# Average pooling over 512 MB: the first load issued as 16 rows and 112 rows

## The chip, the cores and the metric

The kernel runs on one core of a Trainium2 chip. The metric is device time in microseconds (us) of one execution; lower is better. Before the change it is 1552.77 us, the median of 3 runs (1552.75 to 1552.84).

## What is computed

The input x has shape (64, 256, 8192) in float32, which is 536.87 MB. The window and the stride are both 4, so the windows do not overlap, and every output is the mean of four neighbouring numbers of its row:

```
out_len = (length - kernel_size) // stride + 1
for i in range(out_len):
    start = i * stride
    output[:, :, i] = np.mean(x[:, :, start : start + kernel_size], axis=2)
```

The output is (64, 256, 2048) in float32, 134.22 MB. Each input byte is read once, and there are three additions and one multiplication for each output.

## The kernel before, in words

Since 8192 is a multiple of 4, no window crosses the end of a row, and the kernel treats x as one flat array. It cuts it into 64 blocks of 128 x 16384 numbers (`xb`, 8.39 MB each): 128 rows, one for each partition of the on-chip memory, and 64 KB in each row. The rows of a block follow one another in DRAM without gaps. There are two input buffers, `xt0` and `xt1`, each of which holds one block, and two output buffers, `ot0` and `ot1`, each of which holds the results of two blocks.

Four queues do the work, and the order on each of them is written out by hand, with semaphores between them:

- **SP** issues the loads (`load`, L61 to L64), at first blocks 0 and 1, one right after the other with no wait between (L69 and L70). After that it issues the load of block i+2 into the buffer of block i once VectorE has read that buffer (semaphore `free`). Each load adds 16 to the semaphore `full[k]` of its buffer.
- **VectorE (DVE)** waits for `full[k]`, adds neighbours (L75: 16384 numbers of each row to 8192, into the first half of the same buffer) and adds neighbours again (L77: to 4096, into the output buffer).
- **ScalarE (ACT)** multiplies two blocks' sums by 1/4 at a time (L93), and its DMA queue stores them (L96, `stored[q]`).
- After 60 blocks in the loop (L115 on) four blocks follow one by one. The last one is loaded in two halves (`TAIL`, L112), so that the last additions and the last store are short.

The DMA work is done by 16 DMA engines that all queues share. The trace records each packet that they move. Of a load of 128 rows there are 128 packets of 65536 bytes, one for each row, eight for each engine; of a store of two blocks there are 256 packets of 16384 bytes.

At the start, before the loop, SP's two loads stand in front of the barrier that all engines pass on the way in (L71). The first wait of VectorE in the loop is the one for `full[0]`.

Of the kernel before, what the change touches and what calls it, by code (L numbers as in the profile page):

```python
# [1 line left out]

# [4 lines left out]


FULL = 16384
PAIR = 2  # L10
ROUND = 2 * PAIR

TAIL = (8192, 8192)


@with_exitstack
def kernel(
    ctx: ExitStack,
    tc: tile.TileContext,
    x: bass.AP,  # L20
    kernel_size: bass.AP,
    stride: bass.AP,
    out: bass.AP,
):
    nc = tc.nc
    K, S = int(kernel_size), int(stride)
    assert K == S == 4
    B, C, L = x.shape
    assert L % K == 0
    P = nc.NUM_PARTITIONS  # L30
    dt = x.dtype
    add, mult = mybir.AluOpType.add, mybir.AluOpType.mult

    M = FULL // K
    blocks = B * C * L // P // FULL
    loop = blocks - ROUND
    assert blocks * P * FULL == B * C * L and blocks % ROUND == 0 and sum(TAIL) == FULL
    xb = x.rearrange("b c l -> (b c l)").rearrange("(n p m) -> n p m", p=P, m=FULL)
    ob = out.rearrange("b c l -> (b c l)").rearrange("(n p m) -> p n m", p=P, m=M)


    xt0 = ctx.enter_context(nc.sbuf_tensor([P, FULL], dt))
    xt1 = ctx.enter_context(nc.sbuf_tensor([P, FULL], dt))
    ot0 = ctx.enter_context(nc.sbuf_tensor([P, PAIR * M], dt))
    ot1 = ctx.enter_context(nc.sbuf_tensor([P, PAIR * M], dt))
    xt, ot = [xt0, xt1], [ot0, ot1]


    full = [nc.alloc_semaphore(f"full{k}") for k in range(2)]
    piece = [nc.alloc_semaphore(f"piece{k}") for k in range(len(TAIL))]  # L50
    free = nc.alloc_semaphore("free")
    summed = nc.alloc_semaphore("summed")
    summed_last = nc.alloc_semaphore("summed_last")
    scaled = nc.alloc_semaphore("scaled")
    scaled_last = nc.alloc_semaphore("scaled_last")
    stored = [nc.alloc_semaphore(f"stored{k}") for k in range(2)]

    def take(engine, sem, n):
        engine.wait_ge(sem, n).then_inc(sem, -n)  # L59

    def load(i, k):  # L61
        d = nc.sync.dma_start(out=xt[k][:, :], in_=xb[i])
        d.then_inc(full[k], 16)
        return d  # L64

    for k in range(2):
        tc.no_tile_sem_insts.add(load(k, k).ins.name)  # L69
    tc.close()  # L70
    tc.compile()  # L71

    def sums(t, o):
        w = t.shape[1]
        nc.vector.tensor_tensor(out=t[:, : w // 2], in0=t[:, ::2], in1=t[:, 1::2], op=add)  # L75
        nc.vector.drain()
        return nc.vector.tensor_tensor(  # L77
            out=o, in0=t[:, : w // 2 : 2], in1=t[:, 1 : w // 2 : 2], op=add
        )

    def pair(i, q, ahead):

        for k in range(PAIR):
            take(nc.vector, full[k], 16)
            if k == 0:
                take(nc.vector, stored[q], 16)
            sums(xt[k][:, :], ot[q][:, k * M : (k + 1) * M]).then_inc(free, 1)
            take(nc.sync, free, 1)
            if k == 1:
                nc.sync.sem_inc(summed, 1)  # L90
            ahead(k)
        take(nc.scalar, summed, 1)
        nc.scalar.mul(ot[q][:, :], ot[q][:, :], 1.0 / K).then_inc(scaled, 1)  # L93
        take(nc.scalar, scaled, 1)
        o = ot[q][:, :].rearrange("p (n m) -> p n m", n=PAIR)
        nc.scalar.dma_start(out=ob[:, bass.ds(i, PAIR), :], in_=o).then_inc(stored[q], 16)  # L96


    zero = nc.const_aps.tensor(0.0, [P, 1], dt)
    nc.scalar.mul(ot[0][:, :1], zero, 1.0).then_inc(stored[0], 16)  # L100
    nc.scalar.sem_inc(stored[1], 16)

    edges = [sum(TAIL[:i]) for i in range(len(TAIL) + 1)]
    pieces = list(zip(edges[:-1], edges[1:]))
    xe, oe = xb[blocks - 1], ob[:, blocks - 1, :]

    def ahead_of_last(k):
        if k == 0:
            load(blocks - 2, 0)
        else:  # L110
            for sem, (a, b) in zip(piece, pieces):
                nc.sync.dma_start(out=xt[1][:, a:b], in_=xe[:, a:b]).then_inc(sem, 16)  # L112

    engines = (mybir.EngineType.SP, mybir.EngineType.DVE, mybir.EngineType.Activation)
    with nc.Fori(0, loop // ROUND, 1, engines=engines) as r:  # L115
        for q in range(2):
            i = r * ROUND + q * PAIR
            pair(i, q, lambda k: load(i + (PAIR + k), k))

    for k in range(PAIR):
        o = ot[0][:, k * M : (k + 1) * M]
        take(nc.vector, full[k], 16)
        if k == 0:
            take(nc.vector, stored[0], 16)
        sums(xt[k][:, :], o).then_inc(free, 1)
        take(nc.sync, free, 1)
        nc.sync.sem_inc(summed, 1)
        ahead_of_last(k)  # L130
        take(nc.scalar, summed, 1)
        if k == 0:
            nc.scalar.mul(o, o, 1.0 / K).then_inc(scaled, 1)  # L133
            take(nc.scalar, scaled, 1)
            nc.scalar.dma_start(out=ob[:, loop, :], in_=o).then_inc(stored[0], 16)
        else:
            nc.scalar.mul(o, o, 1.0 / K).then_inc(scaled_last, 1)  # L137
            take(nc.sync, scaled_last, 1)
            nc.sync.dma_start(out=ob[:, loop + 1, :], in_=o).then_inc(stored[0], 16)

    take(nc.vector, stored[1], 16)
    take(nc.vector, full[0], 16)
    o = ot[1][:, :M]
    sums(xt[0][:, :], o).then_inc(summed_last, 1)
    take(nc.scalar, summed_last, 1)
    nc.scalar.mul(o, o, 1.0 / K).then_inc(scaled_last, 1)  # L146
    take(nc.sync, scaled_last, 1)
    nc.sync.dma_start(out=ob[:, blocks - 2, :], in_=o).then_inc(stored[1], 16)


    for sem, (a, b) in zip(piece, pieces):
        o = ot[1][:, M + a // K : M + b // K]
        take(nc.vector, sem, 16)
        sums(xt[1][:, a:b], o).then_inc(summed_last, 1)
        take(nc.scalar, summed_last, 1)
        nc.scalar.mul(o, o, 1.0 / K).then_inc(scaled, 1)  # L156
        take(nc.scalar, scaled, 1)
        nc.scalar.dma_start(out=oe[:, a // K : b // K], in_=o).then_inc(stored[1], 16)
    take(nc.sync, stored[0], 32)
    take(nc.sync, stored[1], 16 * (1 + len(TAIL)))  # L160


# [1 line left out]
_INS = ['x', 'kernel_size', 'stride']  # L164
_OUTS = [((64, 256, 2048), 'float32')]

_NUMBERS = {'kernel_size': 4, 'stride': 4}


# [26 lines left out]
```

## Time and profile before

| what | value |
|---|---|
| median of 3 runs | 1552.77 us |
| the profiled execution | 1553.16 us |
| its span, from the first to the last instruction | 1551.8 us |
| around the span | 1.36 us |
| DVE busy | 839.9 us (54%) |
| ACT busy | 227.0 us (15%) |
| DMA, queue of SP (q1), share of 16 engines | 80.5% |
| DMA, queue of ACT (q10), share of 16 engines | 19.6% |
| first load issued by SP | 0.74 us |
| first packet of it starts | 1.77 us |
| its 16 completions | 22.03 to 22.86 us |
| first DVE instruction | 23.11 us |

The times of single events are counted from the start of the span. A transfer has landed when all 16 of its completions, one of each DMA engine, have come in. A packet is put down with its whole size at one moment, so that windows of a few us can show more than the engines can move; windows of 10 us and more do not suffer much from that.

### The profile page before, as it was taken

What the parts mean: (1) busy time and instruction counts of PE and PEld (TensorE: products, weight loads), DVE (VectorE), ACT (ScalarE), POOL (GpSimd) and SP (SyncE); (2) the same over time, 40 slices, a digit from 0 to 9 for tenths busy, and PEclk for the clock granted to TensorE, in tenths of its full rate; (3) what the DMA queues carried; (4) which work ended last, traced back from release to release, by engine and by line L of the source; (5) the groups of instructions that cost most, each with busy time, mean ns of one, the idle gap of its engine ahead of it and who ended that gap; (6) DMA issues with size and microseconds to landing.
All of it is one profiled execution on the core that took longest, in us unless ns stands there. A gap on an engine that the chain in (4) does not pass through costs nothing. (4 is left out here: it accounts for less than half of the span.)

```text
span 1551.8 us, 942 instructions
## 1 busy us (share of the span) xinstructions
DVE 839.9 (54%) x130; ACT 227.0 (15%) x37; POOL 0.2 (0%) x4
## 2 busy tenths in 40 slices
DVE  3645646456465564654646546455464554645546
ACT  0111011110111101111011110111101111011111
POOL 0000000000000000000000000000000000000000
DMA  9999999999999999999999999999999999999999
GB/s 414 419 444 441 417 439 432 439 441 416 433 432 439 446 434 417 432 433 446 439 436 434 413 440 439 439 432 438 414 439 439 432 439 438 416 437 432 439 432 413
DMA packets 18240, 671.10 MB, mean 432 GB/s; under 512 B 1600, under 2 KB 1600, under 8 KB 1600
## 3 DMA queue, kind: packets, MB, share of 16 engines
q1 hardware_dynamic: 9648, 541.07, 80.5%
q10 hardware_dynamic: 8592, 130.03, 19.6%
HBM read 536.87 MB, written 134.22 MB: 432 GB/s over the span
## 5 line engine op out<-in xcount | busy, mean ns | idle before, releaser
L75 DVE TENSOR_TENSOR xt<-xt 128x8192 f32<-128x8192 f32 (+1 forms) x65 | 556.5, 8561 | 699.4 <-DVEq L59 699.4
L93 ACT ACTIVATE ot<-ot 128x8192 f32<-128x8192 f32 x30 | 210.9, 7029 | 1246.2 <-ACTq L59 1246.2
L77 DVE TENSOR_TENSOR ot<-xt 128x4096 f32<-128x4096 f32 (+1 forms) x65 | 283.4, 4360 | 4.9
L146 ACT ACTIVATE ot<-ot 128x4096 f32<-128x4096 f32 x1 | 3.6, 3616 | 20.6 <-ACTq L59 20.6
L137 ACT ACTIVATE ot<-ot 128x4096 f32<-128x4096 f32 x1 | 3.6, 3616 | 20.3 <-ACTq L59 20.3
L133 ACT ACTIVATE ot<-ot 128x4096 f32<-128x4096 f32 x1 | 3.6, 3616 | 17.4 <-ACTq L59 17.4
L156 ACT ACTIVATE ot<-ot 128x2048 f32<-128x2048 f32 x2 | 3.8, 1909 | 12.1 <-ACTq L59 12.1
L100 ACT ACT_TABLE_LOAD x1 | 1.3, 1283 | 2.4 <-PEq L71 2.4
L100 ACT ACTIVATE ot<-const-float32-0.0 128x1 f32<-128x1 f32 x1 | 0.2, 202 | 0.0
L177 POOL MEMSET const-bfloat16-1.0<- 128x1 bf16 x1 | 0.1, 102 | 0.0
L177 POOL MEMSET const-uint8-127<- 128x1 uint8 x1 | 0.1, 102 | 0.0
L177 POOL MEMSET const-float32-0.0<- 128x1 f32 x1 | 0.1, 99 | 0.2 <-issue 0.2
L177 POOL MEMSET const-float32-1.0<- 128x1 f32 x1 | 0.1, 99 | 0.0
## 6 DMA issues: line engine op xcount, KB each, us to landing
out_dram<-ot ACTq DMA_DIRECT2D x30, 4096.0 KB, 51.7
xt<-in_x_dram SPq DMA_DIRECT2D x2, 4096.0 KB, 29.9
out_dram<-ot SPq DMA_DIRECT2D x2, 2048.0 KB, 27.2
out_dram<-ot ACTq DMA_DIRECT2D x1, 2048.0 KB, 45.3
out_dram<-ot ACTq DMA_DIRECT2D x2, 1024.0 KB, 9.1
xt<-in_x_dram SPq DMA_DIRECT2D x63, 34.7
```

Source lines behind the costliest of these rows:

```text
L75: nc.vector.tensor_tensor(out=t[:, : w // 2], in0=t[:, ::2], in1=t[:, 1::2], op=add)
L77: return nc.vector.tensor_tensor(out=o, in0=t[:, : w // 2 : 2], in1=t[:, 1 : w // 2 : 2], op=add)
L93: nc.scalar.mul(ot[q][:, :], ot[q][:, :], 1.0 / K).then_inc(scaled, 1)
L100: nc.scalar.mul(ot[0][:, :1], zero, 1.0).then_inc(stored[0], 16)
L133: nc.scalar.mul(o, o, 1.0 / K).then_inc(scaled, 1)
L137: nc.scalar.mul(o, o, 1.0 / K).then_inc(scaled_last, 1)
L146: nc.scalar.mul(o, o, 1.0 / K).then_inc(scaled_last, 1)
L156: nc.scalar.mul(o, o, 1.0 / K).then_inc(scaled, 1)
L177: nc = _bacc.Bacc("TRN2", target_bir_lowering=False, num_devices=1)
```

## The change

The first load, block 0 into `xt0`, becomes two transfers on the same queue: the first 16 rows (`head`, 1 MB, one row of 64 KB for each of 16 engines) and the other 112 rows (`rest`, 7.34 MB). They are issued by SP without a wait between them, and the load of block 1 follows as before. The head has a semaphore of its own, `first`. VectorE waits for it once ahead of the loop, and `full[0]` is raised by the rest alone. All later loads are as they were.

```diff
+ENGINES = 16
...
+    first = nc.alloc_semaphore("first")
...
-    for k in range(2):
-        tc.no_tile_sem_insts.add(load(k, k).ins.name)
+
+    head = nc.sync.dma_start(out=xt[0][:ENGINES, :], in_=xb[0, :ENGINES])
+    rest = nc.sync.dma_start(out=xt[0][ENGINES:, :], in_=xb[0, ENGINES:])
+    head.then_inc(first, 16)
+    rest.then_inc(full[0], 16)
+    for d in (head, rest, load(1, 1)):
+        tc.no_tile_sem_insts.add(d.ins.name)
     tc.close()
     tc.compile()
...
+    take(nc.vector, first, 16)
     engines = (mybir.EngineType.SP, mybir.EngineType.DVE, mybir.EngineType.Activation)
     with nc.Fori(0, loop // ROUND, 1, engines=engines) as r:
```

`take(engine, sem, n)` waits until the semaphore has reached n and then takes n off it.

## The prediction, as put on record before the run

> **What bounds the kernel now.** I read the page first, then the groups kept apart by shape, the timeline of the first 60 us, and the windows of both ends.
>
> ```profile
> DVE 839.9 (54%) x130; ACT 227.0 (15%) x37; POOL 0.2 (0%) x4
> DMA  9999999999999999999999999999999999999999
> HBM read 536.87 MB, written 134.22 MB: 432 GB/s over the span
> ```
>
> No engine that computes is busy for more than 54% of the span, and the DMA engines are busy in every one of the 40 slices. The kernel is bound by moving bytes, all the way through. The packet records say it more closely. Each of the 16 DMA engines has an equal share: 504 packets of 64 KB (2.418 us each for nearly all), 16 of 32 KB (1.213), 504 of 16 KB (0.611) and 16 of 8 KB (0.309). That is 1218.7 + 19.4 + 307.9 + 4.9 = 1550.9 us for each engine, while from the first packet (1.77 us) to the end of the span there are 1550.0 us; neighbouring packets overlap by a few ns. So an engine has practically no idle time, and an engine that loses time early has nowhere to win it back.
>
> ```profile
> 0.74 98.45 SPq L62 DMA_DIRECT2D xt<-in_x_dram  x6
> 2.40 1.28 ACT L100 ACT_TABLE_LOAD   x1 [2.40 <-PEq L71]
> 23.11 8.69 DVE L75 TENSOR_TENSOR xt<-xt 128x8192 f32<-128x8192 f32 x1 [23.11 <-DVEq L59]
> 42.32 8.69 DVE L75 TENSOR_TENSOR xt<-xt 128x8192 f32<-128x8192 f32 x1 [6.01 <-DVEq L59]
> ```
>
> SP issues the first load at 0.74 us; VectorE has nothing to do until 23.11, when block 0 has landed, and until 42.32, when block 1 has. The distance, 19.21 us, is about eight packets of 2.418 us (19.34), so the two loads run one behind the other on engines that are always full.
>
> ```profile
> 0.00:10.00 10.00, 0.00 (x0) 1.49 (x2) 0.20 (x4) 1.00 0.98 393
> 10.00:20.00 10.00, 0.00 (x0) 0.00 (x0) 0.00 (x0) 1.00 1.01 439
> ```
>
> The columns are window, length, busy DVE, ACT and POOL, clock, DMA share and GB/s. Of the first 10 us, only about 1 us is short of the full rate (393 against 432 to 439).
>
> **The change part by part.** The sum is made against the profiled execution's 1553.16 us; its span is 1551.8 with 1.36 around it. The median of the runs, 1552.77, is 0.39 lower, so I take 0.4 off at the end. "Within 0.2%" is 3.1 us here, about what a measurement of this kernel can tell from no change.
>
> *One more DMA on SP.* A load's issue takes SP 0.333 us (median of 63, from 0.332 to 0.426). The head is issued when the whole load was, the rest 0.33 later, and the load of block 1 another 0.33 later, as is the barrier behind it. Block 1's packets are not wanted before the engines are through with block 0 at some 22 us, and the barrier is waited for by engines that are idle until 23 us. This costs nothing. Without that cover it would be 0.33 us. The head gives each engine one packet of 2.4 us, so the rest, 0.33 us behind, is in the queue before the engines run dry.
>
> *One more wait on VectorE*, for `first`, ahead of the loop. Behind it stands the wait for `full[0]`, in an engine with 23.11 us of idle time. The head runs ahead of the rest on the same queue. Nothing.
>
> *An earlier start.* The first packet starts 1.03 us after the issue, and one of the 16 engines starts its first packet 0.60 us after the last of the others, 1.02 after the first. If 16 rows are prepared faster than 128, the engines could begin sooner. The gain is between 0 and 1.03 less the 0.33 of the issue itself, 0.7 us. The nearest row speaks for little: the first packets of all engines end within 0.83 us of one another, the late starter among them, and all but that one took 2.93 to 3.51 us instead of 2.418, so they waited for data rather than for their own start. I take 0.
>
> *Sixteen neighbouring rows at once.* This is the disputed cost. In a full load the 16 engines have 128 partitions to write, and each packet takes 2.418 us with the others running, so nothing there collides. With the head, all 16 engines write into the first 16 partitions at the same moment, which no transfer of this trace does. How fast 16 neighbouring partitions can take in data is not in any row, so I bound it. Sixteen engines at 64 KB in 2.418 us are 27.1 GB/s each, 434 together, which the 432 of the page nearly reach with every engine at the same steady pace. That looks like as many ways in as engines, each serving 128 / 16 = 8 partitions. If every engine's way leads anywhere, the head takes one packet's time, 2.42 us, and costs nothing. If the 8 partitions of a way are neighbours, 16 rows have two ways for 16 engines, and the head takes 8 x 2.418 = 19.3 us instead of 2.4, which costs 16.9. Between those ends, with the ways dealt out in smaller groups, are four ways: 4 x 2.418 = 9.67 us, 7.25 lost. Neither end has a row on its side. In doublings (one, two, four or eight packets' time) the middle lies between two and four; I take four, because the even pace of full loads needs some order in which neighbours belong together.
>
> [...]
>
> *The rest, 7 rows for each engine.* A full load gives each engine 8 rows and they never collide. Seven rows each, starting at row 16, shift every engine's share against that division, so some engines must share a way for some of their packets. The bounds are 0 (the shares are dealt out so as not to collide) and four packets' time, 9.7 us, for the slowest engine, a bit over half of its seven packets at half speed. I take half of that, two packets, 4.84 us. The slowest engine decides, since a load lands when its last engine is done, and since it has its full share of later work left.
>
> [...]
>
> *What comes later.* Block 1 is again a full load without collisions, so nothing is added there, but nothing is given back: the late engine's share of 1550.9 us is still to be done. In the last window of the trace (1540 to 1552) the rate is 375 GB/s, 57 below the mean, which is 12 x 57 / 432 = 1.6 us of slack at most, and it lies behind the chain of the last additions, the last multiplication and the last store. VectorE's first two blocks start later by the same amount as the data and wait again for the next.
>
> The sum: 0 + 0 + 0 + 7.25 + 4.84 = +12.1 us, 1553.16 + 12.1 = 1565.3 for a profiled execution, 1565 as a median of runs.
>
> **The rivals.**
>
> *It costs nothing.* The way into the memory does not care which partitions are neighbours, or the 16 rows are given to the engines so that they do not collide. Then only the issue and the start are left: 1552.8 with 0.7 less to 0.3 more, 1552.1 to 1553.1. For it speaks that the bytes, their number of packets and the work of each engine are exactly the same, and that the trace has no row with a slowed packet but the first ones. Against it speaks that nothing in the trace ever puts all engines on neighbouring rows. It decides if the head's packets take 2.4 to 3.5 us. This is the rival on the other side of "slower".
>
> *Clearly faster.* To be faster by 3.1 us it would have to win more than the whole dead time ahead of the first packet, 1.77 us; the rest of the span is full. It would need a better rate in the steady state, from engines that have been set apart in time; a rate 0.2% up would do, 1550 us or less. No row of the trace promises that.
>
> *Few engines serve the head.* If eight rows always go to an engine, the head falls to two engines with 8 packets each, and if the rest is spread evenly all the same, these two have 8 + 7 = 15 packets instead of 8: 7 x 2.418 = 16.9 us, 1553.2 + 16.9 - 0.4 = 1569.7. The page's equal work of all engines in 128-row transfers neither supports nor excludes it.
>
> *Every sixteenth row to an engine.* If the rest is dealt out like cards, all engines are on 16 neighbouring rows in each of seven further rounds, and with four ways each round loses 7.25 us: 8 x 7.25 = 58 us, 1611. Full loads dealt in the same way would have to collide in every round too, and after the first round their packets take 2.418 us; this speaks against it.
>
> **How the numbers follow.** Collision in the head, with a rest that collides in part: 0.56, at 1565, from 1556 (head alone with a factor under 3) to 1570. Nothing: 0.31, at 1552.8. Two engines for the head: 0.05, at 1569.7. Dealt like cards: 0.05, at 1611. Clearly faster: 0.03. So slower has 0.56 + 0.05 + 0.05 = 0.66, the same 0.31, faster 0.03. The range must reach to the case of no cost, since 0.31 is more than may be left out, so it goes from 1551.9 to 1571, the upper bound of the sum (1552.8 + 16.9 = 1569.7, and a little). What is left out is the clearly faster, the cards, and part of the first case. The likeliest case's own range is 1556 to 1571.
>
> **What would show it.** If the step is right, the 16 packets of 64 KB of the head take 5 to 20 us each in the packet records, with about 10 the likeliest, the rate of the first 10 us falls from 393 GB/s to some 100 to 250, and the first DVE instruction moves from 23.11 to about 35 us. Its distance to the third (L75 on block 1) need not stay 19.2, as early engines have begun block 1. The rest's packets then show times over 2.5 us in part. Later windows are as before, and the last store is late by the same amount. If the head is free, the first DVE instruction stays between 22.4 and 23.5 and all packets are near 2.4 after the first round. If fewer engines serve the head, its packets take 2.4 to 3 us one after another, and the completions of `first` come in on two steps. A first DVE instruction that is late with an end that is not would show slack that I have not found.

## The result and the profile after

The changed kernel takes 1573.95 us (median of 4 runs, 1573.81 to 1574.23); the kernel before took 1552.8 us beside it (median of 4 runs). The ratio is 1.0135, 95% interval [1.0122, 1.0147]. The change makes the kernel slower by 21 us, 9 more than the 12 that were forecast; the time lies above the forecast's upper end, 1571.

From the page of the changed kernel:

```profile
span 1572.5 us, 944 instructions
...
DVE 839.9 (53%) x130; ACT 227.0 (14%) x37; POOL 0.2 (0%) x4
...
GB/s 213 422 419 437 433 436 438 435 433 429 433 434 440 433 434 428 433 439 434 433 428 433 436 436 433 428 433 434 438 433 433 431 433 437 433 433 432 433 432 403
...
HBM read 536.87 MB, written 134.22 MB: 427 GB/s over the span
```

Bytes and busy times are those of before. The one slice that stands out is the first (39 us): 213 GB/s instead of 414. After it the kernel runs at its old rate. The timeline shows which transfer that is:

```profile
0.74 0.40 SPq L71 DMA_DIRECT2D xt<-in_x_dram  x1
1.20 0.41 SPq L72 DMA_DIRECT2D xt<-in_x_dram  x1
1.66 95.46 SPq L64 DMA_DIRECT2D xt<-in_x_dram  x4
...
44.65 8.69 DVE L82 TENSOR_TENSOR xt<-xt 128x8192 f32<-128x8192 f32 x1 [44.65 <-DVEq L61]
...
63.88 8.69 DVE L82 TENSOR_TENSOR xt<-xt 128x8192 f32<-128x8192 f32 x1 [6.04 <-DVEq L61]
```

L71 is the head, L72 the rest, L64 a full load. VectorE starts on block 0 at 44.65 us instead of 23.11, which is 21.54 later, and on block 1 at 63.88 instead of 42.32, 21.56 later. So block 0 costs all of it and block 1 adds nothing. The windows, with the same columns as before:

```profile
0.00:10.00 10.00, 0.00 (x0) 1.49 (x2) 0.20 (x4) 1.00 0.92 118
10.00:20.00 10.00, 0.00 (x0) 0.00 (x0) 0.00 (x0) 1.00 0.95 197
20.00:30.00 10.00, 0.00 (x0) 0.00 (x0) 0.00 (x0) 1.00 1.15 315
30.00:40.00 10.00, 0.00 (x0) 0.00 (x0) 0.00 (x0) 1.00 0.92 210
40.00:50.00 10.00, 5.35 (x1) 0.00 (x0) 0.00 (x0) 1.00 1.00 406
```

The engines are busy nearly all the time (DMA share 0.92 to 1.15) and in the first 40 us move between three tenths and three quarters of what they did. They are not idle; their packets are slow. The packet records name no engine, but sorted by their start they fall into rounds of 16, one packet for each engine. The head's 16 packets took 7.5 to 8.8 us, where the first 16 packets of the kernel before took 2.4 to 3.5, and the last of its completions came at 13.10 us. The seven rounds of the rest, 2.42 us each in a full load, had medians of 5.5, 4.6, 3.1, 3.8, 4.5, 4.6 and 4.5 us, and its last completion came at 44.40.

### The profile page after: what moved, and what is told of

It reads as the page before. It is cut to its first block, busy times and chain, and to the rows that moved or that the text cites. A ratio compares the mean times of both kernels' runs of the same rounds, so it can differ in the third digit from the quotient of the medians.

```text
span 1572.5 us, 944 instructions
## 1 busy us (share of the span) xinstructions
DVE 839.9 (53%) x130; ACT 227.0 (14%) x37; POOL 0.2 (0%) x4
## 5 line engine op out<-in xcount | busy, mean ns | idle before, releaser
L164 ACT ACTIVATE ot<-ot 128x2048 f32<-128x2048 f32 x2 | 3.8, 1909 | 12.2 <-ACTq L61 12.2
```

## The experiments

Three theories were set against each other. **WAYS**: it matters where the data land; engines that write into neighbouring partitions at the same time slow one another. **SOURCE**: it matters what the engines read at the same time. **CUT**: a transfer of fewer rows, or one more transfer, is slow by itself.

**Probes: fifteen loads, one at a time.** Each is an extra load into `xt0` ahead of block 0, and SP waits for each, so that the next starts when the one before has landed. Every probe ran once, in a single execution.

```diff
+    def done(d):
+        d.then_inc(probe, 16)
+        take(nc.sync, probe, 16)
+    done(io(out=xt[0][:, :], in_=xb[0]))
+    done(io(out=xt[0][:16, :], in_=xb[0, :16]))
+    done(io(out=xt[0][16:, :], in_=xb[0, 16:]))
...
```

> Fifteen extra loads into the first input buffer run one by one ahead of block 0, SP waiting for each; only issue to landing of each is read, and the result of the kernel is as before. In the changed kernel the head took 12.4 us from issue to landing. Three theories. [...] SOURCE: engines that read neighbouring rows of DRAM disturb one another. CUT: any transfer of fewer than 128 rows is slow. From issue to landing, with 2.8 us for start and completion (22.1 - 8 x 2.418 of the first load before): 128 rows 22 by all. 16 rows to partitions 0-15: 12.5 by all. From every eighth source row: WAYS 12.5, SOURCE 5.2, CUT 12.5. [...] 112 rows to partitions 16 on: 29 to 34 by all; to partitions 0 on: the same by WAYS, as is the source shifted. [...] 128 rows by 2048 columns: 5.3 by WAYS and SOURCE, more by CUT.

| line | rows, to partitions, from source rows | issue to landing, us |
|---|---|---|
| L118 | 128, all | 21.9 |
| L119 | 16, 0-15, 0-15 | 11.6 |
| L120 | 112, 16-127, 16-127 | 33.2 |
| L121 | 16, 0-15, every eighth | 11.4 |
| L122 | 16, every eighth, 0-15 | 7.6 |
| L123 | 16, every eighth, every eighth | 7.6 |
| L124 | 16, 3 step 7, 0-15 | 7.0 |
| L125 | 16, 0 step 7, 0-15 | 7.0 |
| L126 | 112, 0-111, 0-111 | 33.0 |
| L127 | 112, 16-127, 0-111 | 34.5 |
| L128 | 96, 0-95, 0-95 | 32.0 |
| L129 | 64, 0-63, 0-63 | 22.8 |
| L130 | 64, every second, 0-63 | 12.4 |
| L131 | 32, 0-31, 0-31 | 12.2 |
| L132 | 128 x 2048 columns | 4.6 |

The times can be read off the timeline of SP's queue, where each start is the landing of the probe before it plus the nearly 0.1 us that SP takes to go on (8 of its 16 lines):

```profile
23.39 0.35 SPq L119 DMA_DIRECT2D xt<-in_x_dram  x1
35.12 0.31 SPq L120 DMA_DIRECT2D xt<-in_x_dram  x1
68.40 0.31 SPq L121 DMA_DIRECT2D xt<-in_x_dram  x1
79.91 0.62 SPq L122 DMA_DIRECT2D xt<-in_x_dram  x1
87.56 0.50 SPq L123 DMA_DIRECT2D xt<-in_x_dram  x1
...
209.15 0.50 SPq L129 DMA_DIRECT2D xt<-in_x_dram  x1
232.08 0.52 SPq L130 DMA_DIRECT2D xt<-in_x_dram  x1
244.59 0.32 SPq L131 DMA_DIRECT2D xt<-in_x_dram  x1
```

L129 and L130 move the same 64 rows of the source. Into 64 neighbouring partitions they need 22.8 us, into every second partition 12.4. SOURCE falls: with the same source the place of landing changes the time, 11.6 against 7.6 (L119 and L122), and with the same place the source changes little or nothing (11.6 and 11.4; 7.6 and 7.6; the 112 rows, L120 and L127, 33.2 and 34.5). CUT falls too: 64 rows can go at full speed (12.4 is four packets of 2.418 and the 2.8 of start and completion). WAYS is left. One range was narrowly missed: L127 took 34.5 (29 to 34 expected). And neighbours are not all of it: 16 rows to every eighth or every seventh partition (L122 to L125) took 7.0 to 7.6 us, where one packet of 2.418 and the 2.8 make 5.2, and with 0 step 7 all 16 packets were slow (4.26 to 5.02 us).

**The split by columns.** The whole of the change's form, semaphores, wait and one more DMA, with 128 rows in both parts.

```diff
-    head = nc.sync.dma_start(out=xt[0][:ENGINES, :], in_=xb[0, :ENGINES])
-    rest = nc.sync.dma_start(out=xt[0][ENGINES:, :], in_=xb[0, ENGINES:])
+    head = nc.sync.dma_start(out=xt[0][:, :2048], in_=xb[0, :, :2048])
+    rest = nc.sync.dma_start(out=xt[0][:, 2048:], in_=xb[0, :, 2048:])
```

> The first load is split by columns instead of rows: 128 rows by 2048 columns, then 128 rows by 14336, the semaphores and the wait as in the change. CUT: a second transfer costs by itself, so some 10 to 21 us slower. WAYS and SOURCE: all rows of both transfers are spread as in a full load, so 1552.8 within 1 us.

Measured: 1553.03 us against 1553.0, ratio 1.0001 [0.9992, 1.001]. One more transfer, wait and semaphore cost nothing that can be measured.

```profile
0.74 0.39 SPq L69 DMA_DIRECT2D xt<-in_x_dram  x1
1.19 0.42 SPq L70 DMA_DIRECT2D xt<-in_x_dram  x1
1.66 34.91 SPq L63 DMA_DIRECT2D xt<-in_x_dram  x2
...
22.75 8.69 DVE L80 TENSOR_TENSOR xt<-xt 128x8192 f32<-128x8192 f32 x1 [22.75 <-DVEq L60]
```

VectorE even starts 0.36 us earlier than before (22.75 against 23.11), but the end does not move with it.

**Two halves of neighbouring rows.**

```diff
+    head = nc.sync.dma_start(out=xt[0][:64, :], in_=xb[0, :64])
+    rest = nc.sync.dma_start(out=xt[0][64:, :], in_=xb[0, 64:])
```

> The first load is split into rows 0-63 and rows 64-127. [...] CUT, with a price for each transfer below 128 rows as the head's 7: 1560 to 1567. If shares are dealt so that nothing collides: 1552.8.

Measured: 1573.7 us, ratio 1.0133 [1.0118, 1.0149], 20.7 more than before, above the range of CUT. It is what the first probes give, where 64 neighbours took 22.8 - 12.4 = 10.4 us longer than 64 rows to every second partition: two times that is 20.8. Its windows show half the rate (210 GB/s, where the kernel before has 393 to 439), steadily, until block 0 is in and VectorE starts:

```profile
0.00:10.00 10.00, 0.00 (x0) 1.49 (x2) 0.20 (x4) 1.00 1.00 210
10.00:20.00 10.00, 0.00 (x0) 0.00 (x0) 0.00 (x0) 1.00 1.02 210
20.00:30.00 10.00, 0.00 (x0) 0.00 (x0) 0.00 (x0) 1.00 1.01 210
30.00:40.00 10.00, 0.00 (x0) 0.00 (x0) 0.00 (x0) 1.00 1.02 210
...
44.20 8.69 DVE L80 TENSOR_TENSOR xt<-xt 128x8192 f32<-128x8192 f32 x1 [44.20 <-DVEq L60]
```

**The rest first, then the head.**

```diff
+    rest = nc.sync.dma_start(out=xt[0][16:, :], in_=xb[0, 16:])
+    head = nc.sync.dma_start(out=xt[0][:16, :], in_=xb[0, :16])
```

> The same 112 rows and 16 rows in the other order, the rest first. If each of the two has its own price (rest 14.4, head 7.0 as in the changed kernel), the sum stays: 1574 within 2 us, with the rest landing about 34 us after its issue. If the rest is slow only because the head before it has set the engines apart in time, it lands at 22 to 25 us and the time is about 1560.

Measured: 1574.19 us, ratio 1.0138 [1.0122, 1.0153]. The rest landed 35.2 us after its issue, where about 34 was expected if it has its own price and 22 to 25 if not.

```profile
45.17 8.69 DVE L80 TENSOR_TENSOR xt<-xt 128x8192 f32<-128x8192 f32 x1 [45.17 <-DVEq L60]
```

Each part has its own price, and their order does not matter; the rest is not slow because of the head before it.

**Probes by steps.** Open was why 16 rows to spread partitions took 7.0 to 7.6 us and not 5.2, with all 16 packets slow at 0 step 7. The diff is that of the first probes, with other places.

> Probes as before: extra loads into the first input buffer, one at a time ahead of block 0, all but two of 16 rows (64 KB each), told apart only by the partitions they land in. [...] 16 neighbours from 32: 11.6 as from 0.

By the packet records of each probe (median of the 16 packets, range, and issue to landing):

| partitions | packet, us | landing |
|---|---|---|
| 11 step 7 | 2.68 (2.42 to 3.28) | 5.3 |
| 3, 4, 15, 18 step 7; 28 step 4 | 2.9 to 3.1, slowest 4.2 to 5.0 | 6.8 to 7.4 |
| 0, 1, 16 step 7; 24 step 4; 4 step 6 | 4.2 to 4.9, fastest 3.7 to 4.5 | 7.2 to 7.6 |
| 34 step 6 | 4.54 (4.29 to 5.06) | 7.6 |
| 16 step 4 | 4.74 (4.04 to 5.09) | 7.3 |
| 32 rows, every fourth | 2.42, after a first round of 3.3 | 8.1 |
| 32 to 47 | 8.77 (7.94 to 9.25) | 11.7 |

```profile
23.29 0.62 SPq L119 DMA_DIRECT2D xt<-in_x_dram  x1
28.68 0.51 SPq L120 DMA_DIRECT2D xt<-in_x_dram  x1
35.99 0.51 SPq L121 DMA_DIRECT2D xt<-in_x_dram  x1
...
125.34 0.35 SPq L133 DMA_DIRECT2D xt<-in_x_dram  x1
137.13 0.83 SPq L63 DMA_DIRECT2D xt<-in_x_dram  x2
```

L119 is 11 step 7: 16 rows of 64 KB land in 5.3 us, and the next probe goes out 0.1 later. L133, 16 neighbours, needs 11.7. Eight of the probes have the same step of 7 and differ only in where they begin, and they are of three kinds. From 11 the median is 2.68 us. From 3, 4, 15 and 18 it is 2.9 to 3.1: 14 of the 16 packets take 3.5 us or less, and two are slow. From 0, 1 and 16 all 16 are slow (1 and 16 step 7: fastest packets 3.7 and 3.9). In all seven probes of this third kind the fastest packet took 3.7 us and the slowest 5.6, so none kept the 2.42 of a full load. What it is about a place that decides, no run here shows. Issue to landing alone would not have told the last two kinds apart, since the slowest packet sets it: 6.8 to 7.4 us with two slow packets, 7.2 to 7.6 with 16.

**Even and odd rows.**

```diff
+    head = nc.sync.dma_start(out=xt[0][::2, :], in_=xb[0, ::2])
+    rest = nc.sync.dma_start(out=xt[0][1::2, :], in_=xb[0, 1::2])
```

> The first load is split by rows again, into 64 even rows and 64 odd rows (each to the partitions of the same number), two transfers back to back with the semaphores and the wait of the change. [...] If splitting by rows itself costs, or source rows 128 KB apart do: near the 1573.7 of the halves with neighbouring rows.

The 64 rows to every second partition had landed in 12.4 us, against 22.8 for 64 neighbours, so if the place decides, the time was to stay at 1552.8 within 1 us. Measured: 1553.49 us against 1553.07, ratio 1.0003 [0.9994, 1.0013].

```profile
23.38 8.69 DVE L80 TENSOR_TENSOR xt<-xt 128x8192 f32<-128x8192 f32 x1 [23.38 <-DVEq L60]
```

It is the halves again, by rows, with the same number of bytes in each, and 20 us of difference come from which rows go together.

**Eight transfers of 16 neighbours.**

```diff
+    parts = [
+        nc.sync.dma_start(out=xt[0][16 * j : 16 * j + 16, :], in_=xb[0, 16 * j : 16 * j + 16])
+        for j in range(8)
+    ]
+    for d in parts[:7]:
+        d.then_inc(first, 16)
+    parts[7].then_inc(full[0], 16)
...
+    take(nc.vector, first, 7 * 16)
```

> The first load is split into eight transfers of 16 neighbouring rows. [...] By the probe's 11.6 - 2.8 = 8.8 us for each: 51 us more, 1604. If the price of a head is paid once, at the start: 1560 to 1575.

Measured: 1608.1 us, ratio 1.0355 [1.0337, 1.0372], 55 us more. That lies between the sum from the probe (51) and eight times the 7.25 that the prediction estimated for the head (58).

```profile
78.53 8.69 DVE L83 TENSOR_TENSOR xt<-xt 128x8192 f32<-128x8192 f32 x1 [78.53 <-DVEq L60]
```

Each group of 16 neighbours pays on its own, about 6.9 us.

**96 rows and 32 rows, and four times every fourth row.** The first tests whether the landings of the probes add up to the price of a split, the second whether a split into spread rows is free however often it is made. By the probes the 96 rows landed in 32.0 us instead of 6 x 2.418 + 2.8 = 17.3, which is 14.7 more, and 32 neighbours in 12.2 instead of 2 x 2.418 + 2.8 = 7.6, which is 4.6 more. The 32 rows to every fourth partition landed in 8.1, so the four were to cost nothing but their issue, 1553 to 1554.

```diff
+    head = nc.sync.dma_start(out=xt[0][:96, :], in_=xb[0, :96])
+    rest = nc.sync.dma_start(out=xt[0][96:, :], in_=xb[0, 96:])
```

> The first load is split into rows 0-95 and rows 96-127, two transfers back to back, else as in the change. A test of the account by sums of what the probes gave. [...] Together +19.3, 1572. [...]

```diff
+    parts = [
+        nc.sync.dma_start(out=xt[0][j::4, :], in_=xb[0, j::4])
+        for j in range(4)
+    ]
+    for d in parts[:3]:
+        d.then_inc(first, 16)
+    parts[3].then_inc(full[0], 16)
...
+    take(nc.vector, first, 3 * 16)
```

> The first load is split by rows into four transfers of 32 rows, each of every fourth row to every fourth partition. [...] If the number of transfers counts, three times the change's price or at least more than 1560.

Measured: 1572.72 us for 96 and 32, ratio 1.0126 [1.0109, 1.0143], within 1 us of the sum; 1554.06 us for the four, ratio 1.0007 [0.9997, 1.0016], which cannot be told from no change. No version beats the kernel before, and none was to be expected: its engines are full from the first microseconds on (DMA share 0.98 in the first 10 us).

## Why the prediction was wrong

*The bound* was right: the kernel moves bytes from end to end, and what a load loses early stays lost. The 21.5 us by which VectorE is late on the first block are still 20.7 in the span at the end (1572.5 against 1551.8). The prediction said that nothing would be given back. In fact 0.8 is: VectorE's fourth block is late by 20.76 (106.12 against 85.36), its third still by 21.56 (83.35 against 61.79). In the kernel before the first store is issued between these two blocks, and 16 packets of 64 KB took about 2.9 us there (at 65.4 us of the span) and 16 about 2.6 (at 72); in the changed kernel no packet after the first of block 1 takes over 2.5 us. Whether that is because its engines have been set apart in time was not tried.

*One more DMA and one more wait* at nothing: right, by the split by columns. Block 1's load goes out at 1.66 us instead of 1.18 and nothing waits for it. *The earlier start* at nothing: right for the end.

*The head*, four packets' time, 7.25 us lost: right in size. The four, though, was the author's estimate, a choice between bounds of one and eight that stood in no row, so that it came out so closely was in part luck; no run shows how many ways there are, or which partitions belong to one. The head landed 12.4 us after its issue, where 16 rows to every seventh partition from 11 on landed in 5.3: 7.1 lost. What is measured is that the time follows the partitions (16 neighbours 11.6, every eighth 7.6) and not the source (11.6 and 11.4, 7.6 and 7.6).

*The rest*, two packets' time, 4.84 us: this is the step that failed. It was "some engines must share a way for some of their packets", bounded at "four packets' time, 9.7 us, for the slowest engine", "a bit over half of its seven packets at half speed". From the landing of the head (13.10) to that of the rest (44.40) it took 31.3 us instead of 7 x 2.418 = 16.9, so 14.4 was lost (13.5 by the medians of its seven rounds, which add up to 30.5), and the bound was wrong as well as the value. The reason is what the bound took for granted: that only some engines are slow, and for some of their packets. In the changed kernel no packet of the rest kept the 2.42 of a full load: in five of the seven rounds the fastest of the 16 took 4.2 to 5.1 us, and in the two others, the third and the fourth, 2.75 and 3.62. The step probes show it for 16 rows alone, where at some places every packet took 3.7 us or more. Which rounds are faster changes with the partitions. In the probe of the rest (L120) they are again the third and the fourth: medians 3.55 and 3.04 us, with 4.5 to 4.7 in the five others. When the 112 rows begin at partition 0 (L126) they are the fourth and the fifth (3.41 and 3.46). In L127, the 112 rows to partitions 16 on from other source rows, the third is fast (3.21), and the fourth only a little faster than the others (4.16). Why these rounds, no run shows.

With 14.4 in the place of 4.84 the prediction's sum is 7.1 + 14.4 = 21.5, which is the shift of VectorE's start (21.54). Landings of single probes, added up in the same way, gave the time of the 96 and 32 rows to within 1 us before it was measured.

*The rivals.* "It costs nothing" falls for this split, but is true of the even and odd rows (1.0003). "Few engines serve the head" falls: the head's 16 packets started within 1.0 us of one another, and all were slow. "Every sixteenth row to an engine" falls: each round of the rest would have been as slow as the head (7.5 to 8.8 us), and they had medians of 3.1 to 5.5 us.

Open is why 16 rows slow all 16 packets at some places and only two or none at others. Open is also by what rule a transfer's rows are dealt to the engines, since the packet records name none.

## What to carry to other kernels

What was measured holds for loads from DRAM with rows of 64 KB on one core. Before such a load is split by rows, look at which partitions the parts fill: every second or every fourth row cost nothing that could be measured here (ratios 1.0003 and 1.0007), while packets to 16 neighbours took up to 3.8 times as long (9.25 us against 2.42), though the engines look busy all the while (DMA share 0.92 in the first 10 us of the changed kernel). A split by columns leaves that alone (1.0001). When a bound is worked out from sharing, ask also what those who do not share will do: here all 16 packets of a round were slow in five of the rest's seven rounds, 4.2 us or more.

## What the runs showed that was not expected

- Among 16 rows to spread partitions the place made the difference: at seven places all the packets were slow, with medians of 4.2 to 4.9 us; at five the median was about 3 (2.42 at the fastest), with two slow packets; at one it was 2.68.
- 64 rows to every second partition land in 12.4 us, 64 neighbours in 22.8, and the 96 neighbours need 32.0, hardly less than 112 (33.2) and 10 us more than 128 (21.9): the fewer rows took longer.
- The rows of the source made little difference or none in the three pairs of probes that differ in them alone (11.6 and 11.4, 7.6 and 7.6; the 112 rows 33.2 and 34.5).
